# Small matrix products of three token mixers in other array forms, and an issue order that plans by tile size

## The chip, the cores and the metric

The kernel runs on one core of one Trainium2 chip, in float32. The metric is the device time of one execution in microseconds. Before the change three runs took 1665.26, 1686.83 and 1694.75 us; their median is 1686.83 us.

A core has five engines with a queue each: PE multiplies matrices (PEld loads its stationary operand), DVE, ACT and POOL do everything elementwise, SP issues DMAs. PE writes to PSUM, of which this kernel uses eight banks of 128 x 512 float32. The PE array can be addressed as a whole (128 rows x 128 columns, written 128\*128 in the profile) or in part (64\*64, 128\*64, 128\*32, 32\*32 and so on); the part is set by how many partitions the stationary operand spans and how many columns it has. This is called the tile size below. A float32 product shows as two matmul instructions in the trace; a float32r product as one.

## The reference, cut to what matters

One decoder layer over 1024 tokens of 1024 channels:

```
h = x * (1 + scale1) + shift1                  # adaLN, from c
z = h @ w_in                                   # 3984 columns
o = concat(HGRN2(z), GLA(z), RWKV7(z)) @ w_out
x = layer_norm(alpha * x + (1 + gate1) * o)
m = square(relu((x * (1 + scale2) + shift2) @ mlp_w_up)) @ mlp_w_down
x = layer_norm(alpha * x + (1 + gate2) * m)
```

HGRN2 (4 heads of 64) and GLA (6 heads) are gated linear attention: within a chunk, scores of queries and keys with decays between them times values, plus the decayed queries times a state. RWKV-7 (6 heads) is a delta rule, done in chunks of 64 tokens with an inverse of a triangular 64 x 64 matrix for each head and chunk.

## The kernel before

**Dense products.** The tokens are cut into two blocks of 512. Every dense product (projections, MLP) is split into high and low parts and done as three float32r matmuls of 512 or 392 columns (helper `mm3`, L1270 to L1272, tile size 128\*128). ACT makes the high part of a weight slab (L1220), DVE the low part (L1221). They write to PSUM banks `dn` (four) and, in the last part, `tn`.

**Mixers.** `mixers` runs over tiles of 128 tokens, four in each block, RWKV-7 a tile ahead of the attention. For a tile, the steps that the change touches are these.
- `rw_prep` makes AR and BK (for both chunks c and pairs of heads p) and their products (L598): for each c, six float32 products of 64 rows (a half of the partitions holds one head) by 128 columns, tile size 64\*128, into two PSUM banks `mr`. BK holds three parts, k, b and a copy of k that ACT makes (L585), so that one contiguous slice gives the rows in the order that head a needs.
- `rw_prep2` transposes BK (L662): 12 transposes of 64 x 128 in four banks, four ACT copies (L664).
- `rw_invert` (L718 to L750, tile size 32\*32) and `rw_chain` (L770, L775, L781) follow; at the end of the second chunk the outputs y: for each head of a pair, and each chunk d, three products AR x SU (L795, 64\*64), then three E x UV (L798, 128\*64), one bank after the other, one ACT copy each (L800).
- `la_attn` makes the scores level by level. At level 64 (`la_blocks`, L512) it does ten products on 64\*64, heads a = 0 and 1 into two banks `ml`, both on the first 64 columns of the array; level 32 (L521) and the five finer ones (L434) are on 128\*32. Each level is POOL, ACT, DVE, PE and a copy. Then the outputs: for each pair of heads one product of the whole array, decayed queries times the state (L475, 128 columns), and four products of 64 columns, scores times values (L482): for each head the first 64 tokens on 64\*64, the last 64 on 128\*64. ACT copies them out (L484). The state update (transposes L491, products L497) ends the tile.

**Order of issue.** Every engine runs its instructions in the order of its queue. Class `Order` lays that order out when the kernel is built, for all five engines: it simulates them with a cost for each instruction (`cost`), keeps for each engine a heap of instructions that are ready, and takes the one of lowest level, then earliest in the program (`pick`). PSUM banks and buffers are counted (`fits`). If few columns went through PE lately by its count (`behind`), a ready dense product goes first. Levels: the mixers of the first block are at 0, its later projections at 0.5, the second block's projection at 2, the MLP at 3 and up; the second block's mixers at 0 to 6.5. So dense products of a later level fill PE wherever the mixers' products are not ready, one instruction at a time. In `cost`, a PE instruction costs its columns over a rate, and two neighbours on different halves of the array cost half.

Of the kernel before, what the change touches and what calls it, by code (L numbers as in the profile page):

```python
# [19 lines left out]
P = 128  # L20
# [22 lines left out]
# buffers of the mixers' tiles  # L43
WKB = 4
LDB = 2
# of raw and split slabs of weights, of split operands; of late raw tiles
RB, WB, AB, LR = 5, 4, 12, 6
# the last of the groups of 128 columns of adaLN that the first sub-layer's shift and scale take
FIRST = 15
# importance (lower first) of the iterations of each block's mixers  # L50
M0 = (0, 0, 0, 0, 0, 0)
M1 = (0, 0, 3.5, 4.5, 5.5, 6.5)
# of the first block's last projections, the other columns of adaLN, the second block's projection, and the
# first chunk of the MLP, each later chunk being one more
L_Z0, L_ADA, L_Z1, L_MLP = 0.5, 3, 2, 3
# chunks of the first block's MLP that the second block's output projection and its products follow
OUT_AT, MOVE_AT = 4, 6
# tiles of the first layer norm and of the MLP's operand that ACT and Pool take
# [6 lines left out]
# levels of the attention between blocks of 32 tokens, and within them  # L65
# [4 lines left out]
# columns of the array of constants  # L70
# [6 lines left out]
# columns of the array of masks  # L77
# [5 lines left out]
# rows of the array of per-channel vectors  # L83
# [36 lines left out]
class Kern:  # L120
# [13 lines left out]
    # importance of what follows: lower is issued first  # L134
# [7 lines left out]
    # activations of one table set after another: a set's work is issued as a group  # L142
# [30 lines left out]
    # banks of RWKV-7 and of the others  # L173
# [18 lines left out]
    # not before the first columns of adaLN  # L192
# [3 lines left out]
    def setup_mixers(self, masks, vecs, wau, alpha_up, g_up, nrm):  # L196
# [15 lines left out]
        # rows over all partitions: gn_g | gn_b  # L212
# [6 lines left out]
        # lower bounds of HGRN2: softmax over the layers, cumsum less the first  # L219
# [9 lines left out]
        # 1 - k_a  # L229
# [3 lines left out]
        # states  # L233
# [6 lines left out]
        # right factors: zero where the heads of a pair do not meet  # L240
# [12 lines left out]
        # gains of the norms of HGRN2 and GLA  # L253
# [4 lines left out]
    def rw_sig(self, i, src):  # L258
# [13 lines left out]
        # norm of k * k_k  # L272
# [10 lines left out]
        # sigmoids  # L283
# [85 lines left out]
    def la_decay(self, s):  # L369
# [9 lines left out]
        # f * 2**60 below 2**-60, f elsewhere  # L379
# [27 lines left out]
    def la_attn(self, s):  # L407
# [4 lines left out]
        for h in H_OUT + H_LEVELS:  # L412
# [16 lines left out]
            # the four blocks of 32 tokens on the four quarters of the array's columns  # L429
# [11 lines left out]
        # the diagonal  # L441
# [13 lines left out]
        # decayed queries and keys  # L455
# [13 lines left out]
        # outputs  # L469
        for p0, p1 in ((0, 3), (3, 5)):  # L470
            n = p1 - p0
            po = self.lps()
            for p in range(p0, p1):
                c0 = (p - p0) * 128
                nc.tensor.matmul(po[:, c0:c0 + 128], qe[:, p, :], St[:, p, :], start=True, stop=False,  # L475
                                 skip_group_check=True)
                for a in range(2):
                    v0 = p * 128 + 64 * a
                    # the first half of the tokens sees no token of the second
                    for t in range(2):  # L480
                        r = slice(0, 64 + 64 * t)
                        nc.tensor.matmul(po[half[t], c0 + 64 * a:c0 + 64 * a + 64], sc[r, 2 * p + a, half[t]],  # L482
                                         V[r, v0:v0 + 64], start=False, stop=True, skip_group_check=True)
            nc.scalar.copy(o[:, 2 * p0:2 * p1, :], po[:, 0:n * 128].rearrange("p (q d) -> p q d", d=64))  # L484
        # state
# [18 lines left out]
    # the large levels block by block  # L504
    def la_blocks(self, h, e, R):
        nc, sc = self.nc, self.sc
        if h == 64:
            pss = [self.lps() for _ in range(2)]
            for p in range(5):
                for a in range(2):  # L510
                    r = slice(64 * a, 64 * a + 64)
                    nc.tensor.matmul(pss[a][0:64, p * 64:p * 64 + 64], e[r, p * 128:p * 128 + 64], R[r, a, p, :],  # L512
                                     start=True, stop=True)
            for a in range(2):
                nc.scalar.copy(sc[0:64, a::2, 64:128], pss[a][0:64, 0:320].rearrange("p (q t) -> p q t", q=5))
            return
# [27 lines left out]
    def rw_prep(self, i, s):  # L544
# [9 lines left out]
        # decays within each chunk of 64  # L554
# [9 lines left out]
        # kk: k * k_k normalized over the head  # L564
# [9 lines left out]
        BK = self.mt([P, 3, 2, 3, 64], "BK")  # L574
# [3 lines left out]
        nc.vector.tensor_tensor(BKm[:, :, 1, :], c6(b), c6(eb), ALU.mult)  # L578
# [5 lines left out]
        nc.vector.tensor_tensor(BKm[:, :, 0, :], c6(k2), c6(eb), ALU.mult)  # L584
        nc.scalar.copy(BKm[:, :, 2, :], BKm[:, :, 0, :])  # L585
# [3 lines left out]
        # products of the chunks: rows b~, k~ of a head of even number, k~, b~ of an odd one  # L589
        s["E"] = []  # L590
        for c in range(2):
# [3 lines left out]
            for p in range(3):  # L595
                for a in range(2):
                    rr = slice(64 * a, 64 * a + 64)
                    nc.tensor.matmul(pxs[a][:, p * 128:(p + 1) * 128],  # L598
                                     BK[rr, p, c, 1 - a:3 - a, :].rearrange("p x t -> p (x t)"),
                                     AR[rr, p, c].rearrange("p x t -> p (x t)"), start=True, stop=True)  # L600
# [6 lines left out]
    def rw_prep2(self, s):  # L607
# [3 lines left out]
        # bonus coefficients  # L611
# [11 lines left out]
        # gate  # L623
# [4 lines left out]
        # v with the tokens on partitions, opposite to the state's and u's half of each pair  # L628
# [25 lines left out]
        # b~ and k~ with the tokens on partitions  # L654
        s["BKT"] = []
        for c in range(2):
            BT = self.mt([P, 2, 3, 64], "BT", 2)
            for a in range(2):
                rr = slice(64 * a, 64 * a + 64)
                pt = self.mps()  # L660
                for p in range(3):
                    nc.tensor.transpose(pt[:, p * 64:(p + 1) * 64],  # L662
                                        BK[rr, p, c, 1 - a:3 - a, :].rearrange("p x t -> p (x t)"), self.ident[rr, rr])
                nc.scalar.copy(BT[:, a], pt[:, 0:192].rearrange("p (q d) -> p q d", d=64))  # L664
            s["BKT"].append(BT)

    # of an array [m, i, n, j] the parts with n = m
# [5 lines left out]
    def rw_base(self, s):  # L673
        nc = self.nc
        # rows of a head; the inverses go where all but the blocks is zero
# [33 lines left out]
    def rw_invert(self, s):  # L709
        nc = self.nc  # L710
        E, TW = s["E"], s["TW"]
        # blocks of 32, a quarter of the array each
# [907 lines left out]
```

## Time and profile before

| | |
|---|---|
| runs | 1665.26, 1686.83, 1694.75 us; median 1686.83 us |
| profiled execution | its span is 1676.5 us; the page gives no other time for it, and the span is 10.3 us less than the median |
| PE busy | 1565.6 us (93%), 11002 matmuls |
| PEld / DVE / ACT / POOL busy | 1220.9 / 1097.7 / 683.0 / 419.1 us |
| granted TensorE clock, mean | 0.928 |
| PE idle just before an instruction of L434, L475, L598, waiting for DVE or ACT | 17.3, 15.4 and 9.6 us in all |

Read it so: PE is the engine that is nearly always busy; the clock of 0.928 is a mean over stretches at full clock (1.0) and stretches at half (0.5). The 40 slices of the page show the clock under 0.9 only between the seventh and the 24th, that is in the two stretches with the mixers (some 210 to 565 us and 690 to 1060 us), and in the last. From 1060 us on there are only dense products.

### The profile page before, as it was taken

Reading aid. Unit: us, or ns where it says so; the run is one execution under the profiler, and the core shown is the slowest. Engines: PE = TensorE matmul, PEld = TensorE weight load, DVE = VectorE, ACT = ScalarE, POOL = GpSimd, SP = SyncE. Lnnn points to the kernel's source line nnn. Section 1 sums busy time; section 2 is a strip of 40 time slices with the busy share of each in tenths; the row PEclk is TensorE's granted clock in tenths of the full one; section 3 lists DMA queues with packets and bytes.
Section 4 is the critical chain, followed back from the end, with each engine's and each line's share of the span. In section 5 each row is a group of like instructions: output and inputs, shape, how many; then the busy total and the mean of one; then the engine's idle time right before and its main releaser. Section 6 shows DMA issues by size and latency. Waiting matters only on the chain.

```text
span 1676.5 us, 29172 instructions
## 1 busy us (share of the span) xinstructions
PE 1565.6 (93%) x11002; PEld 1220.9 (73%) x11002; DVE 1097.7 (65%) x1877; ACT 683.0 (41%) x1415; POOL 419.1 (25%) x561
## 2 busy tenths in 40 slices
PE   6998988999989998889999999999999999999996
PEld 5887766666667876657667676778888888888885
DVE  8796586666657448875857766555766954444477
ACT  3452343444344655544534543442333333333241
POOL 5224054263434132451452624100000000000003
PEclk9999996787879999898959989999999999999998
DMA  9997542313322456522313131444523643333331
GB/s 310 324 335 232 181 134 68 108 51 110 87 65 86 130 176 194 178 63 77 88 37 105 39 101 44 146 132 130 191 95 94 201 144 96 96 97 96 94 120 50
DMA packets 164892, 214.03 MB, mean 128 GB/s; under 512 B 41456, under 2 KB 91792, under 8 KB 164752
## 3 DMA queue, kind: packets, MB, share of 16 engines
q1 hardware_dynamic: 164752, 212.18, 40.5%
q8 instruction: 86, 1.41, 0.3%
q14 instruction: 54, 0.44, 0.1%
HBM read 180.07 MB, written 32.06 MB: 127 GB/s over the span
## 4 chain that ended last, share of the span: by engine, by line
PE 49%; DVE 6%; DMA 1%; issue 1%; ACT 1%; POOL 1%; SPq 0%; DVEq 0%; ACTq 0%; POOLq 0%
PE dn L1272 10%; PE dn L1271 9%; PE dn L1270 9%; PE tn L1272 4%; PE tn L1271 4%; PE tn L1270 4%; PE ml L482 1%; DVE Rs L425 1%; PE ml L475 1%; PE mr L798 1%; PE mr L795 1%; DVE xt L1401 1%; DVE wl L1221 0%; DMA lnr<-in_ln_b_dram 0%; PE ml L434 0%
## 5 line engine op out<-in xcount | busy, mean ns | idle before, releaser
L1220 ACT CAST wh<-raw 128x512 fp32r<-128x512 f32 (+2 forms) x424 | 253.2, 599 | 558.4 <-PE dn L1272 230.7
L1221 DVE TENSOR_TENSOR wl<-raw,wh 128x512 fp32r<-128x512 f32 (+2 forms) x408 | 284.8, 703 | 274.0 <-ACT wh L1220 246.0
L1270 PE MATMUL dn<-wh,ah 128*128 128x512 f32 (+1 forms) x736 | 288.0, 393 | 6.8 <-DVE xt L1417 3.8
L1271 PE MATMUL dn<-wl,ah 128*128 128x512 f32 (+1 forms) x736 | 288.0, 391 | 2.0 <-DVE wl L1221 2.0
L1272 PE MATMUL dn<-wh,al 128*128 128x512 f32 (+1 forms) x736 | 285.1, 394 | 1.8 <-DVE al L1443 1.8
L1270 PE MATMUL dn<-ah,wh 128*128 128x512 f32 x560 | 236.7, 424 | 19.6 <-ACT ah L1263 11.7
L1271 PE MATMUL dn<-al,wh 128*128 128x512 f32 x560 | 236.7, 423 | 3.2 <-DVE al L1221 1.6
L1272 PE MATMUL dn<-ah,wl 128*128 128x512 f32 x560 | 236.8, 424 | 0.0
L1270 PEld LDWEIGHTS dn<-wh,ah 128*128 128x128 f32 x736 | 140.7, 191 | 36.8 <-ACT wh L1220 3.5
L1271 PEld LDWEIGHTS dn<-wl,ah 128*128 128x128 f32 x736 | 140.3, 191 | 29.6 <-DVE wl L1221 3.4
L1272 PEld LDWEIGHTS dn<-wh,al 128*128 128x128 f32 x736 | 140.0, 191 | 29.5 <-DVE al L1443 3.2
L1270 PEld LDWEIGHTS dn<-ah,wh 128*128 128x128 f32 x560 | 111.8, 200 | 44.4 <-ACT ah L1263 11.7
L1271 PEld LDWEIGHTS dn<-al,wh 128*128 128x128 f32 x560 | 112.0, 200 | 30.3 <-DVE al L1264 4.1
L1272 PEld LDWEIGHTS dn<-ah,wl 128*128 128x128 f32 x560 | 111.8, 200 | 23.6 <-issue 0.4
L416 POOL TENSOR_TENSOR ld<-b 128x640 f32<-128x640 f32 x56 | 76.5, 1373 | 138.0 <-PE ml L512 15.3
L1458 DVE TENSOR_TENSOR xt<-xt,dn 128x512 f32<-128x512 f32 x104 | 67.1, 683 | 52.9 <-PE dn L1272 52.8
L1272 PE MATMUL tn<-ah,wl 128*128 128x512 f32 x256 | 100.8, 394 | 0.0
L1271 PE MATMUL tn<-al,wh 128*128 128x512 f32 x256 | 100.2, 391 | 0.0
L1270 PE MATMUL tn<-ah,wh 128*128 128x512 f32 x256 | 99.6, 389 | 0.0
L1518 POOL TENSOR_SCALAR lnm<-lnm 128x1 f32<-128x1 f32 x3 | 2.1, 684 | 328.5 <-DVE lnm L1516 328.5
L425 DVE TENSOR_TENSOR Rs<-ld,Q 64x320 f32<-64x320 f32 x112 | 82.0, 732 | 2.0 <-ACT ld L157 0.6
L1186 DVE SCALAR_TENSOR_TENSOR xt<-xt,xt 128x1024 f32<-128x1024 f32 x48 | 64.2, 1344 | 16.3 <-DMA xt<-in_ada_wt_dram 16.0
(290 smaller groups left out, 2500.9 us busy)
## 6 DMA issues: line engine op xcount, KB each, us to landing
raw<-in_mlp_w_up_dram SPq DMA_DIRECT2D x128, 256.0 KB
raw<-in_mlp_w_down_dram SPq DMA_DIRECT2D x128, 256.0 KB
xt<-in_ada_wt_dram SPq DMA_DIRECT2D x48, 512.0 KB
raw<-in_w_in_dram SPq DMA_DIRECT2D x64, 256.0 KB
raw<-in_w_in_dram SPq DMA_DIRECT2D x48, 192.0 KB
raw<-in_w_out_dram SPq DMA_DIRECT2D x32, 256.0 KB
raw<-in_w_in_dram SPq DMA_DIRECT2D x32, 196.0 KB
raw<-in_xt_dram SPq DMA_DIRECT2D x24, 256.0 KB
```

What stands on the lines that cost most here:

```text
L416: nc.gpsimd.tensor_tensor(ev, bv, bv[:, :, h - 1:h].broadcast_to([P, 5 * nb, 2 * h]), ALU.subtract)
L425: nc.vector.tensor_tensor(Rv[half[a], a], ev[half[a], :, up], qv[half[a], :, up], ALU.mult)
L475: nc.tensor.matmul(po[:, c0:c0 + 128], qe[:, p, :], St[:, p, :], start=True, stop=False, skip_group_check=True)
L482: nc.tensor.matmul(po[half[t], c0 + 64 * a:c0 + 64 * a + 64], sc[r, 2 * p + a, half[t]], V[r, v0:v0 + 64], start=False, stop=True, skip_gr ...
L795: nc.tensor.matmul(py[half[d], p * 64:p * 64 + 64], AR[rr, p, d, 1, :], s["SU"][d][rr, p, a, :], start=(p == 0), stop=False, skip_group_ch ...
L1186: nc.vector.scalar_tensor_tensor(w, w, 1.0, self.cact, ALU.mult, ALU.mult, accum_out=self.sums[:, q:q + 1])
L1220: nc.scalar.copy(hi[:, 0:n], src)
L1221: (eng or nc.vector).tensor_tensor(lo[:, 0:n], src, hi[:, 0:n].bitcast(F32), ALU.subtract)
L1270: nc.tensor.matmul(ps, lh, rh, start=first, stop=False)
L1271: nc.tensor.matmul(ps, lh, rl, start=False, stop=False)
L1272: nc.tensor.matmul(ps, ll, rh, start=False, stop=last)
L1458: nc.vector.tensor_tensor(acc[t][:, cs], acc[t][:, cs], ps, ALU.add)
```

## The change

Five groups of small products change, and the planner. Comments are dropped too, which moves no instruction.

```diff
 la_attn, outputs
-                    # the first half of the tokens sees no token of the second
-                    for t in range(2):
-                        r = slice(0, 64 + 64 * t)
-                        nc.tensor.matmul(po[half[t], c0 + 64 * a:c0 + 64 * a + 64], sc[r, 2 * p + a, half[t]],
-                                         V[r, v0:v0 + 64], start=False, stop=True, skip_group_check=True)
+                    nc.tensor.matmul(po[:, c0 + 64 * a:c0 + 64 * a + 64], sc[:, 2 * p + a, :], V[:, v0:v0 + 64],
+                                     start=False, stop=True, skip_group_check=True)
 la_blocks, level 64
-            pss = [self.lps() for _ in range(2)]
-            for p in range(5):
-                for a in range(2):
-                    r = slice(64 * a, 64 * a + 64)
-                    nc.tensor.matmul(pss[a][0:64, p * 64:p * 64 + 64], e[r, p * 128:p * 128 + 64], R[r, a, p, :],
-                                     start=True, stop=True)
-            for a in range(2):
-                nc.scalar.copy(sc[0:64, a::2, 64:128], pss[a][0:64, 0:320].rearrange("p (q t) -> p q t", q=5))
+            ps = self.lps()
+            for p, j in ((0, 0), (3, 1), (1, 0), (4, 1), (2, 0)):
+                c0 = (p - 3 * j) * 128
+                for m in range(2):
+                    s0 = 64 * j + 32 * m
+                    nc.tensor.matmul(ps[s0:s0 + 32, c0:c0 + 128], e[:, p * 128 + 32 * m:p * 128 + 32 * m + 32],
+                                     R[:, :, p, :], start=True, stop=True)
+            for j, h0, h1 in ((0, 0, 6), (1, 6, 10)):
+                nc.scalar.copy(sc[0:64, h0:h1, 64:128], ps[64 * j:64 * j + 64, 0:64 * (h1 - h0)]
+                               .rearrange("p (q t) -> p q t", t=64))
 rw_prep (BK has two parts now, b first)
-        nc.scalar.copy(BKm[:, :, 2, :], BKm[:, :, 0, :])
...
-                    nc.tensor.matmul(pxs[a][:, p * 128:(p + 1) * 128],
-                                     BK[rr, p, c, 1 - a:3 - a, :].rearrange("p x t -> p (x t)"),
-                                     AR[rr, p, c].rearrange("p x t -> p (x t)"), start=True, stop=True)
+                for x in range(2):
+                    for a in range(2):
+                        rr = slice(64 * a, 64 * a + 64)
+                        r = slice(64, 128) if a ^ x else slice(0, 64)
+                        nc.tensor.matmul(pxs[a][r, p * 128:(p + 1) * 128], BK[rr, p, c, x, :],
+                                         AR[rr, p, c].rearrange("p x t -> p (x t)"), start=True, stop=True)
 rw_prep2
-            for a in range(2):
-                rr = slice(64 * a, 64 * a + 64)
-                pt = self.mps()
-                for p in range(3):
-                    nc.tensor.transpose(pt[:, p * 64:(p + 1) * 64],
-                                        BK[rr, p, c, 1 - a:3 - a, :].rearrange("p x t -> p (x t)"), self.ident[rr, rr])
-                nc.scalar.copy(BT[:, a], pt[:, 0:192].rearrange("p (q d) -> p q d", d=64))
+            pt = self.mps()
+            for p in range(3):
+                nc.tensor.transpose(pt[:, p * 128:(p + 1) * 128], BK[:, p, c].rearrange("p x t -> p (x t)"), self.ident)
+            pt3 = pt[:, 0:384].rearrange("p (q d) -> p q d", d=128)
+            nc.scalar.copy(BT[:, 0], pt3[:, :, 0:64])
+            for x in range(2):
+                nc.scalar.copy(BT[64 - 64 * x:128 - 64 * x, 1], pt3[64 * x:64 * x + 64, :, 64:128])
 rw_chain, outputs
-            for a in range(2):
-                rr = half[a]
-                py = self.mps()
-                for d in range(2):
-                    for p in range(3):
-                        nc.tensor.matmul(py[half[d], ...], AR[rr, p, d, 1, :], s["SU"][d][rr, p, a, :], ...)
-                    for p in range(3):
-                        nc.tensor.matmul(py[half[d], ...], s["E"][d][:, a, p, 64:128], s["UV"][d][:, p, a, :], ...)
-                nc.scalar.copy(...)
+            pys = [self.mps() for _ in range(2)]
+            for p in range(3):
+                for d, a in ((0, 0), (1, 1), (0, 1), (1, 0)):
+                    nc.tensor.matmul(pys[a][half[d], ...], AR[half[a], p, d, 1, :], s["SU"][d][half[a], p, a, :], ...)
+            for a in range(2):
+                for p in range(3):
+                    for d in range(2):
+                        nc.tensor.matmul(pys[a][half[d], ...], s["E"][d][:, a, p, 64:128], s["UV"][d][:, p, a, :], ...)
+                nc.scalar.copy(...)
```

In the planner, `cost` now charges weight loading with a float32 product, 15 ns with a float32r one, and notes the tile size (`mode`) and the parts of the array (`cells`) of each PE instruction; in `run`, a change of tile size waits until all cells are free and adds 130 ns (`SWITCH`), and an instruction on part of the array holds only its cells, the next may go 20 ns later (`ISSUE`). A predicated copy is charged 1.4 times as much. PE instructions of one tile size other than 128\*128 that follow each other in the program with no other engine's instruction between them form a run:

```diff
+    def runs(self):
+        self.run_of, self.mode, self.cells, last = {}, {}, {}, None
+        for k, i in enumerate(self.ins):
+            if self.eng[k] != PE:
+                last = None
+                continue
+            self.cost(k)
+            if self.mode[k] == (P, P):
+                last = None
+            elif last and self.mode[last[0]] == self.mode[k]:
+                last.append(k)
+            else:
+                last = [k]
...
+        for k, r in self.run_of.items():
+            for m in r[1:]:
+                for d, seen in self.after[m].items():
+                    if d < k:
+                        self.after[k][d] = self.after[k].get(d, 0) or seen
 pick
+            if e == PE and run:
+                x = self.rank[run[0]]
+                if x not in ready[e]:
+                    return None
+                run.pop(0)
+                return take(x)
             if e == PE and behind():
...
+            if e == PE and self.now != (P, P):
+                for x in sorted(ready[e]):
+                    if self.mode[x[1]] == self.now and fits(x[1]):
+                        run.extend(self.run_of.get(x[1], ())[1:])
+                        return take(x)
```

So the first of a run waits for the inputs of all of it and for all its PSUM banks (`fits` sums over the run), the run is then issued unbroken, and after it other ready products of the same tile size come before anything else, unless `behind` asks for a dense one.

## Rows read from the trace of the kernel before

**Rows 1.** Busy time by stage (stretch, length, engines' busy us, clock, DMA share, GB/s).
```profile
210.00:565.00 355.00, 323.61 (x3402) 237.95 (x3402) 230.48 (x421) 160.50 (x393) 148.82 (x205) 0.82 0.30 88
...
690.00:1060.00 370.00, 342.65 (x3529) 250.82 (x3530) 259.66 (x451) 178.29 (x413) 151.91 (x200) 0.87 0.24 70
1060.00:1657.00 597.00, 594.10 (x2612) 484.73 (x2611) 351.45 (x555) 196.70 (x325) 10.65 (x11) 1.00 0.39 121
```

**Rows 2.** The same view, one stretch in the first block's mixers.
```profile
275.90:299.00 23.10, 23.09 (x101) 15.54 (x101) 11.59 (x23) 9.65 (x23) 6.68 (x9) 0.51 0.26 80
```

**Rows 3.** Waits of engines between 210 and 565 us (total us, times, longest).
```profile
POOL ld L468 <- PE ml L475: 41.9, 4, 13.1
ACT wp L800 <- PE mr L798: 31.7, 8, 6.4
```

**Rows 4.** Busy time of L482 alone, one stretch for each tile, first and last of eight.
```profile
275.00:290.00 15.00, 8.33 (x40) 0.55 0.28 84
...
1037.00:1050.00 13.00, 5.20 (x40) 0.85 0.17 51
```

**Rows 5.** Timeline of PE (start, length, operation, count): attention outputs, fourth tile.
```profile
553.46 0.49 PE L475 MATMUL ml<-st,ld 128*128 128x128 f32 x2
553.88 1.73 PE L482 MATMUL ml<-V,sc 64*64 64x64 f32 x14
555.54 0.49 PE L475 MATMUL ml<-st,ld 128*128 128x128 f32 x2
```

**Rows 6.** Timeline of PE: attention outputs, first tile.
```profile
282.79 2.70 PE L482 MATMUL ml<-V,sc 64*64 64x64 f32 x14
285.42 0.80 PE L475 MATMUL ml<-st,ld 128*128 128x128 f32 x2
```

**Rows 7.** Timeline of PE: first product off the whole array; last before dense products alone.
```profile
95.81 0.37 PE L291 MATMUL mr<-zm,wau 64*128 64x128 f32 x1
...
1050.44 0.80 PE L497 MATMUL ml<-V,ld 128*64 128x64 f32 x20
1051.17 0.50 PE L1271 MATMUL dn<-al,wh 128*128 128x512 f32 x1
```

**Rows 8.** Timeline of PE: outputs y of RWKV-7, third tile.
```profile
458.34 0.56 PE L795 MATMUL mr<-SU,AR 64*64 64x64 f32 x6
458.82 0.56 PE L798 MATMUL mr<-UV,E 128*64 128x64 f32 x6
```

**Rows 9.** Timeline of PE: small products between dense ones, first tile.
```profile
248.33 0.33 PE L770 MATMUL mr<-SU,E 128*64 128x64 f32 x2
248.59 0.50 PE L1271 MATMUL dn<-al,wh 128*128 128x512 f32 x1
248.93 0.40 PE L1272 MATMUL dn<-ah,wl 128*128 128x512 f32 x1
249.25 0.25 PE L434 MATMUL ml<-Rs,ld 128*32 128x32 f32 x2
249.43 0.56 PE L770 MATMUL mr<-SU,E 128*64 128x64 f32 x10
249.92 0.46 PE L434 MATMUL ml<-Rs,ld 128*32 128x32 f32 x32
250.46 0.56 PE L775 MATMUL mr<-sm,TW 64*64 64x64 f32 x12
```

**Rows 10.** Groups of PE instructions by line and shape (count, busy us, mean ns, idle before).
```profile
L662 PE MATMUL mr<-consts,BK 64*128 64x64 f32 x96 | 15.3, 296 | 0.8 <-ACT BT L664 0.6 <-DVE bon L651 0.3
...
L631 PE MATMUL mr<-consts,zm 128*128 128x128 f32 x24 | 4.6, 308 | 0.0
```

**Rows 11.** Waits of PE over the whole span (total us, times, longest).
```profile
PE mr L598 <- ACT BK L585: 9.6, 4, 3.1
```

**Rows 12.** The instructions of L585 (duration min/median/max in ns).
```profile
L585 ACT COPY BK<-BK x8: 509/512/515, 113.3 to 919.0; 128x384 f32<-128x384 f32 x8
```

**Rows 13.** Timeline of PE: products of the chunks and of level 64, sixth tile.
```profile
813.55 0.94 PE L598 MATMUL mr<-AR,BK 64*128 64x128 f32 x12 [3.14 <-ACT BK L585]
814.42 1.15 PE L512 MATMUL ml<-Rs,ld 64*64 64x64 f32 x20
```

## What the change will do to the time: the prediction

> **What bounds the kernel now.** First the busy times by stage [rows 1]: PE is busy for 324 of 355 us in the mixers of the first block, for 343 of 370 us in those of the second, for 594 of 597 us in the dense stretch behind. No other engine comes near: DVE has 230 and 260 us. So the kernel is as long as PE's work, and the question for every edit is what it takes from PE. The second thing to see there is the clock: 0.82 and 0.87 in the two mixer stretches against 1.00 in the dense one. The clock has two levels here, 1.2 and 2.4 GHz, so 0.82 means that 36% of 355 us (128 us) ran at the lower one, and 0.87 that 26% of 370 us (96 us) did: 224 us in all. Rows 2 [rows 2] show what PE did in such a stretch: busy for 23.09 of 23.10 us, with 101 instructions, most of them small products.
>
> Next the waits [rows 3]: in the first block POOL waited 41.9 us for L475 and ACT 31.7 us for L798. Slow small products thus hold the mixers' own chain as well as PE.
>
> Last the timeline of PE. In the attention outputs 14 instructions of L482, which alternate between two tile sizes, take from 553.88 to 555.54, 119 ns each, and L475's pair between them 0.42 us [rows 5]; in the first tile, at the lower clock, 14 take 2.63 us, 188 ns each [rows 6]. And each stretch on one tile size has a fixed cost: two instructions of L770 hold PE for 0.26 us, ten for 0.49 us, so one more costs 0.03 us and the stretch itself 0.20 us; the dense product after it takes 0.34 us where its neighbours take 0.23 [rows 9]. Counted over all of PE's instructions, the array changes size 861 times, first at 95.81 us, and 1051.17 us is the last change of the mixers [rows 7]; 585 stretches are off the whole array, 155 of them of L482, 82 of L795 and L798, 30 of L662.
>
> **The parts.** Eight tiles of tokens; prices at full clock, then weighted.
>
> *Attention outputs (L475, L482).* A tile now: 40 x 0.119 + 5 x 0.42 = 6.9 us at full clock, x 188/119 = 10.8 us at the lower. The eight stretches of L482 had clocks from 0.52 to 0.98, mean 0.70, the first and last 0.55 and 0.85 [rows 4], so 60% at the lower: 8 x (0.4 x 6.9 + 0.6 x 10.8) = 74 us. After, 20 instructions of the whole array with 64 columns take the place of the 40, and L475's ten have no change of size around them. No row has such an instruction. From above: L475's 210 ns with 128 columns and a change on either side. From below: L497, 64 columns on half-width tiles, 20 in 0.73 us, 37 ns [rows 7]. I take half of L475's, 105 ns, for it streams half the columns through the same whole array, and 150 ns for L475 itself: 20 x 0.105 + 10 x 0.15 = 3.6 us, 7.2 at the lower clock. With the share as now 46 us, with 30% at the lower 37 us: between them, **-32 us**. Ends: +7 us (210 ns for all, share as now) and -55 us (37 ns).
>
> *Outputs y (L795, L798).* Six instructions take 0.48 us [rows 8], 80 ns each, and all six of one group lie on the same part of the array. 48 a tile: 3.8 us. After, 24 on 64\*64 go round four parts, then 24 on 128\*64 round two. L775 (64\*64, two parts) takes 0.56 us for 12, 47 ns, L770 (128\*64, two parts) 49 ns [rows 9]: 2.3 us. With the stage's clock (some 30% at the lower, factor 1.17) 8 x 1.5 x 1.17 = **-14 us**; ends 0 and -21 us, the latter if the four parts give L434's 17 ns (32 in 0.54 us [rows 9]). Both banks `mr` are now held at once; before, the second could be filled while ACT copied the first. That is one copy more to wait for in a tile, under 0.5 us, covered by dense products.
>
> *Transposes (L662).* 96 instructions cost 15.3 us, 159 ns each; 48 of the whole array at L631's 4.6/24 = 192 ns [rows 10] make 9.2: **-6 us**. ACT gets six copies a tile for four and loses L585's; it is busy for 160 of 355 us [rows 1], so I cost that at nothing; uncovered it would be 1 us a tile.
>
> *The copy L585.* It lasts 0.51 us [rows 12] and PE waited for it four times, 9.6 us [rows 11]; the product on DVE that it copies ends just before it, and that is what is late next. So not 9.6 but 4 x 0.5 = **-2 us**.
>
> *Chunk products (L598) and level 64 (L512).* L598 takes 0.87 us for 12 now; after, 24 of 128 columns go round four parts. L434, 32 columns on four parts, 17 ns, is the lower bound, four times that, 68 ns, the upper; at 40 ns they cost 0.96 us: **0**, ends -7 and +12 us over 16 groups. L512 takes 54 to 57 ns for each of 20 [rows 13]; after, the same count with 128 columns on four parts, 0.8 for 1.1 us: **-3 us**, ends -6 and +2. It holds one bank `ml` instead of two and has the tile size of the next levels.
>
> *Order.* The forms take away 267 stretches and bring back 16; 318 others stay. In the program a tile's small products come in some 27 groups, 216 for eight tiles: about 100 stretches fewer at 0.20 us, 0.31 where a dense product stood behind: **-20 us**; ends -45 (groups of one size meet often) and +10. This adds a wait: a run's first instruction waits for the last input of the run and for all its banks. Behind it in PE's queue stands everything, dense products too, but the planner puts a run there only when it sees the inputs as ready. The same simulation also lays out DVE, ACT, POOL and SP anew, the DMAs of the inverses and of the weight slabs among them; DMA is at 0.30 and 0.24 of its time in these stretches [rows 1], which leaves room, so nothing for that; without that room a weight slab's wait would be added to PE.
>
> *Clock.* Small products lose about a quarter of their time. If the 224 us at the lower clock shrink alike, by 56 us, 28 us come back; half of it is in the terms above. **-15 us**; the end on the good side is -50.
>
> **Sum.** -32 - 14 - 6 - 2 - 3 - 20 - 15 = -92 us. The profiled span is 1676.5 us, 10.3 us under the median of the runs; the same step from the median gives 1687 - 92 = **1595 us**. With the ends of single terms this case covers 1540 to 1630 us.
>
> **The rivals.**
>
> *The whole array is not cheaper.* Against the step on L482 stands a trace price too: 64-column products on part of the array run at 37 ns (L497), a third of what I charge for the whole. If those 210 ns of L475 are the real price, the term turns from -32 to +7: 1595 + 39 = 1634 us. Chance 0.12. The Trainium skill, "TensorEngine Tiling (Array Packing)", section "Theoretical Speedup", has it that way: a dimension of 64 or less, put on tiles, goes up to twice as fast, so L482 and L662 should have stayed on parts. By that rule the time would be this rival's. L482's 119 ns, no quicker than my price for the whole, speaks against it where sizes alternate.
>
> *PE's freed time goes idle in the first block.* There the dense products left to fill are few, and a chain of POOL, ACT, DVE and PE sets the pace; DVE is busy for 65% of it. Then only the second block, filled by the MLP, pays: half of 92, 1641 us. For it: PE's 31 idle us in that stretch. Against it: rows 3, where POOL and ACT wait for just these products. Chance 0.13.
>
> *Unbroken small products hold the clock down.* Place: the two mixer stretches. Rows 2 show PE busy all the time and still at half clock, so busy alone doesn't keep the clock; runs that no dense product may break could make such stretches longer. Each further us at the lower clock costs half a us of work. The other terms give 77 us; it takes 154 us more at the lower clock to eat them, 222 more (446 of the 725 us) to be slower by 2%. At 480 us: (480 - 224)/2 - 77 = +51, 1738 us. Against it: the rule that puts dense products first when few columns went through stands ahead of the new one, and the worst stretches are those of L482, which shrink. Chance 0.08.
>
> *The order gives it back.* The planner's new prices move everything; if the new order fits the chip worse by some 80 us of stalls, the time is that of before, 1665 to 1690 us. Idle time of PE in the mixer stretches is 59 us now; it would have to double. Chance 0.12.
>
> **The numbers.** Forecast 0.55, rivals 0.12, 0.13, 0.08, 0.12. A measurement of this kernel tells about 2% (34 us) from no change: 1653 us. The forecast, most of the first rival and two thirds of the second lie below: faster 0.74. The fourth and what is left of the others: same 0.20; slower 0.06. The range 1520 to 1660 leaves out the third and nearly all of the fourth, and the good ends of the clock and order terms.
>
> **What would show it.** L482's successor with 160 instructions of 128\*128 at about 105 ns; y in 2.3 us a tile; changes of tile size well under half of 861; clock above 0.85 in the first mixer stretch; both mixer stretches shorter by 35 to 50 us, the dense stretch after them unchanged. I am wrong in the mechanism if PE's idle time in the mixers grows by more than 30 us, or the clock falls.

## The result, and the profile after

The changed kernel takes 1602.80 us (median of four runs, 1601.35 to 1604.74); the kernel before, run beside it, 1680.66. The ratio is 0.956, with a 95% interval of 0.951 to 0.961: faster by 4.4%. The forecast was 1595 us, range 1520 to 1660. The profiled span went from 1676.5 to 1603.0 us.

The busy times by stage (stretch, length, busy us of PE, PEld, DVE, ACT, POOL, clock, DMA share, GB/s) of the changed kernel, against [rows 1]; first, of the kernel before, the stretch between its mixers, which [rows 1] leaves out:

```profile
565.00:690.00 125.00, 113.62 (x572) 90.02 (x570) 86.22 (x151) 65.03 (x127) 37.09 (x59) 1.00 0.63 196
...
210.00:500.00 290.00, 235.50 (x3273) 177.64 (x3272) 233.36 (x417) 157.14 (x384) 151.81 (x206) 0.88 0.34 99
500.00:640.00 140.00, 132.24 (x698) 109.10 (x697) 87.21 (x152) 72.11 (x143) 37.60 (x59) 0.99 0.60 182
640.00:975.00 335.00, 279.79 (x3481) 215.24 (x3480) 256.69 (x447) 173.60 (x404) 149.52 (x198) 0.89 0.28 81
975.00:1583.00 608.00, 602.36 (x2651) 489.77 (x2648) 356.15 (x564) 203.56 (x339) 12.47 (x12) 1.00 0.38 120
```

The mixer stretches shrank by 65 and 35 us, the dense stretch behind them is as full as before. That is more than the whole span lost, because dense work moved out of the mixers (577 and 701 dense instructions there became 479 and 666): the stretch between them has 698 instructions of PE in 140 us where it had 572 in 125, and the last one 2651 where it had 2612. But see what became of PE in the mixers: it is idle for 54.5 of 290 and 55 of 335 us, where it was 31 and 27. DVE has the same work in less time and is busy for 80% of the first stretch (65% before). PE's longest waits (total us, times, longest) are for DVE. The first was 17.3 us before; the other two are new, for before PE waited 0.8 us in front of L662 and 9.6 for ACT's copy in front of L598:

```profile
PE ml L434 <- DVE Rs L425: 22.2, 18, 3.9
PE mr L661 <- DVE bon L652: 19.0, 5, 6.6
PE mr L600 <- DVE BK L585: 13.6, 6, 3.2
```

The changed groups, by line and shape (count, busy us, mean ns of one, idle before), first of the kernel before:

```profile
L482 PE MATMUL ml<-V,sc 64*64 64x64 f32 x160 | 32.5, 297 | 0.0
L482 PE MATMUL ml<-V,sc 128*64 128x64 f32 x160 | 32.3, 302 | 0.0
...
L475 PE MATMUL ml<-st,ld 128*128 128x128 f32 x80 | 25.3, 412 | 15.4 <-DVE ld L460 15.4
...
L798 PE MATMUL mr<-UV,E 128*64 128x64 f32 x192 | 22.9, 256 | 0.0
L598 PE MATMUL mr<-AR,BK 64*128 64x128 f32 x192 | 22.5, 337 | 9.9 <-ACT BK L585 9.6
L795 PE MATMUL mr<-SU,AR 64*64 64x64 f32 x192 | 22.2, 250 | 2.3 <-DVE UV L778 2.3
```

and of the changed kernel, where L480 is the old L482, L600 the old L598, L661 the old L662, L800 the old L798:

```profile
L480 PE MATMUL ml<-V,sc 128*128 128x64 f32 x160 | 23.6, 268 | 0.0
L600 PE MATMUL mr<-AR,BK 64*64 64x128 f32 x384 | 19.8, 311 | 16.9 <-DVE BK L585 13.6 <-DVE BK L579 3.2
L475 PE MATMUL ml<-st,ld 128*128 128x128 f32 x80 | 19.3, 336 | 3.5 <-DVE ld L460 3.5
L661 PE MATMUL mr<-consts,BK 128*128 128x128 f32 x48 | 11.1, 354 | 20.1 <-DVE bon L652 19.0 <-ACT BT L665 1.0
L512 PE MATMUL ml<-Rs,ld 128*32 128x128 f32 x160 | 10.0, 367 | 0.7 <-DVE Rs L425 0.6
L800 PE MATMUL mr<-UV,E 128*64 128x64 f32 x192 | 8.1, 236 | 0.0
L795 PE MATMUL mr<-SU,AR 64*64 64x64 f32 x192 | 6.1, 246 | 1.3 <-DVE SU L786 1.3
```

The mean of one is its length from start to end, and neighbours overlap, so prices are read from starts. From here on each PE instruction is charged the time to the start of the next, less the idle time in front of that one. The timeline of the changed kernel (start, length, count), attention outputs of the fourth tile at full clock:

```profile
489.89 0.44 PE L475 MATMUL ml<-st,ld 128*128 128x128 f32 x2
490.17 0.56 PE L480 MATMUL ml<-V,sc 128*128 128x64 f32 x4
490.56 0.44 PE L475 MATMUL ml<-st,ld 128*128 128x128 f32 x2
490.84 0.56 PE L480 MATMUL ml<-V,sc 128*128 128x64 f32 x4
491.20 0.42 PE L1328 MATMUL dn<-wh,al 128*128 128x392 f32 x1
```

Four of L480 take 0.36 to 0.39 us, 90 to 98 ns each; a pair of L475 0.28. And RWKV-7's outputs, against [rows 8]:

```profile
468.63 0.85 PE L795 MATMUL mr<-SU,AR 64*64 64x64 f32 x24
469.42 0.92 PE L800 MATMUL mr<-UV,E 128*64 128x64 f32 x24
470.26 0.50 PE L1326 MATMUL dn<-ah,wh 128*128 128x512 f32 x1
```

24 in 0.79 us and 24 in 0.84, 33 and 35 ns each, in two stretches where there were eight or more.

Added up that way over the whole span, with every kernel of the study (medians and ratios from the runs, each ratio against the kernel before as it ran beside that kernel, with medians of 1677 to 1681 us; the other columns from the one profiled execution, in us of PE; "dense" are the instructions of `mm3`, "small" all others, "lower" is the time at the lower clock):

| kernel | median | ratio, 95% interval | dense | small | idle | lower | changes of tile size |
|---|---|---|---|---|---|---|---|
| before | 1680.66 | 1 | 1234 | 331 | 96 | 243 | 861 |
| changed | 1602.80 | 0.956 (0.951-0.961) | 1216 | 220 | 152 | 161 | 345 |
| forms only | 1604.98 | 0.954 (0.950-0.959) | 1229 | 261 | 101 | 168 | 614 |
| planner only | 1673.93 | 0.998 (0.996-1.000) | 1241 | 270 | 147 | 195 | 678 |
| changed, no runs | 1648.03 | 0.980 (0.977-0.984) | 1250 | 249 | 133 | 168 | 621 |
| changed, old attention outputs | 1637.41 | 0.975 (0.972-0.979) | 1220 | 254 | 152 | 195 | 542 |
| changed, new PE prices alone | 1671.88 | 0.994 (0.990-0.998) | 1273 | 270 | 113 | 212 | 760 |
| changed, no preference | 1595.85 | 0.950 (0.945-0.956) | 1214 | 218 | 147 | 146 | 363 |
| changed, other prices raised | 1547.99 | 0.921 (0.916-0.927) | 1213 | 204 | 116 | 101 | 355 |
| forms only, other prices raised | 1571.54 | 0.935 (0.929-0.942) | 1216 | 247 | 91 | 97 | 643 |
| changed, old y | 1624.01 | 0.969 (0.964-0.974) | 1227 | 240 | 147 | 184 | 413 |
| changed, DVE's price raised | 1563.12 | 0.932 (0.928-0.936) | 1208 | 206 | 130 | 96 | 360 |
| changed, prices raised threefold | 1573.41 | 0.939 (0.934-0.943) | 1220 | 212 | 128 | 155 | 337 |
| other prices raised, no preference | 1551.41 | 0.925 (0.920-0.930) | 1211 | 205 | 120 | 99 | 366 |

So the 73.5 us between the first two spans are 111 us less of small products, 18 less of dense ones, and 56 us more of idle time.

### The profile page after: what moved, and what is told of

Same layout as the page of the kernel before. It is cut to its first block, busy times and chain, and to the rows that moved or that the text cites. A ratio compares the mean times of both kernels' runs of the same rounds, so it can differ in the third digit from the quotient of the medians.

```text
span 1603.0 us, 29184 instructions
## 1 busy us (share of the span) xinstructions
PE 1436.2 (90%) x10986; PEld 1144.5 (71%) x10986; DVE 1099.2 (69%) x1877; ACT 687.0 (43%) x1423; POOL 418.0 (26%) x561
## 4 chain that ended last, share of the span: by engine, by line
PE 51%; DVE 11%; POOL 6%; DMA 3%; issue 3%; ACT 3%; SPq 0%; DVEq 0%; POOLq 0%; ACTq 0%
PE dn L1328 11%; PE dn L1326 11%; PE dn L1327 11%; PE tn L1328 5%; PE tn L1327 5%; PE tn L1326 4%; DVE Rs L425 1%; POOL btw L699 1%; POOL btm L697 1%; DVE wl L1277 1%; DVE zm L269 1%; POOL ld L416 1%; DMA lnr<-in_ln_b_dram 1%; DVE ld L420 1%; DVE xt L1457 1%
## 5 line engine op out<-in xcount | busy, mean ns | idle before, releaser
L1277 DVE TENSOR_TENSOR wl<-raw,wh 128x512 fp32r<-128x512 f32 (+2 forms) x408 | 289.0, 712 | 339.7 <-ACT wh L1276 304.6
L1328 PE MATMUL dn<-ah,wl 128*128 128x512 f32 x560 | 233.2, 418 | 2.2 <-DVE wl L1277 2.1
L425 DVE TENSOR_TENSOR Rs<-ld,Q 64x320 f32<-64x320 f32 x112 | 77.2, 690 | 3.3 <-ACT ld L157 2.3
L157 ACT ACTIVATE ld<-ld 128x320 f32<-128x320 f32 (+1 forms) x120 | 55.0, 491 | 42.9 <-POOL ld L416 41.0
```

Of the source, the lines that this page charges most:

```text
L157: ins = nc.scalar.activation(out, in_, func, **kw)
L425: nc.vector.tensor_tensor(Rv[half[a], a], ev[half[a], :, up], qv[half[a], :, up], ALU.mult)
L1277: (eng or nc.vector).tensor_tensor(lo[:, 0:n], src, hi[:, 0:n].bitcast(F32), ALU.subtract)
L1328: nc.tensor.matmul(ps, ll, rh, start=False, stop=last)
```

## The experiments

**Forms and planner apart.** The first kernel has the new forms and class `Order` of before, the second the forms of before and the new `Order`.

> The new array forms of the five groups, with the planner of before. In the changed kernel the five groups take 67.5 us of PE against 159.9 before (start to start), so about 92 us less, and PE's idle time is 152 us against 96. Theory (the forms bring most of the gain; idle time gives part back): L475 and L480 together under 40 us, the y group under 25 us, 1615 to 1640 us. Rival (the order of issue brings most of it, the forms would still be cut up by changes of tile size): the y group over 30 us, 1650 us or more.

> The new planner with the array forms of before. Theory (forms first): the attention outputs keep their alternation of tile sizes, L475 and L482 stay near 75 us; the other groups save some 20 to 30 us, y a part more; 1640 to 1670 us. Rival (order first): 1625 us or less.

The forms alone give the whole gain: 1604.98 us; the two ratios, 0.954 and 0.956, can't be told apart. They save 71 us of small products: L475 with L480 34.3 us (76.3 before), y 20.4 (39.4), L661 6.6 (13.2); L600 and L512 hardly move. Groups of this kernel:

```profile
L480 PE MATMUL ml<-V,sc 128*128 128x64 f32 x160 | 28.2, 308 | 0.0
L475 PE MATMUL ml<-st,ld 128*128 128x128 f32 x80 | 21.4, 365 | 19.5 <-DVE ld L460 19.4
L795 PE MATMUL mr<-SU,AR 64*64 64x64 f32 x192 | 11.9, 251 | 2.4 <-DVE SU L786 1.5 <-DVE UV L779 0.9
L800 PE MATMUL mr<-UV,E 128*64 128x64 f32 x192 | 10.9, 254 | 0.0
```

The planner alone gives 0.2%: it saves 61 us of small products and pays 51 us of idle time and 7 us of dense time. Both times came outside what I expected, the forms 10 us below it, the planner 4 us above. Nor did L475 and L482 stay near 75 us with the planner alone: they took 57.4, for fewer of them ran at the lower clock (75 of 400 against 228). On top of the forms it does the same again: 41 us of small and 13 of dense products against 51 us of idle time.

**Is a group's PE time worth its time?** The old attention outputs, then the old outputs y, put back into the changed kernel.

```diff
-                    nc.tensor.matmul(po[:, c0 + 64 * a:...], sc[:, 2 * p + a, :], V[:, v0:v0 + 64], ...)
+                    for t in range(2):
+                        r = slice(0, 64 + 64 * t)
+                        nc.tensor.matmul(po[half[t], c0 + 64 * a:...], sc[r, 2 * p + a, half[t]], V[r, v0:v0 + 64], ...)
```

> The changed kernel with the attention outputs of before (two products of 64 columns for each head on 64*64 and 128*64 instead of one on the whole array). Theory (term of 47 us, PE bound): 30 to 50 us slower than the changed kernel, 1633 to 1653 us. Rival (freed PE time went idle in the mixers, so giving it back costs little): under 15 us slower, with idle time falling by 25 us or more.

> The changed kernel with the outputs y of RWKV-7 in the order of before (three products of one head and chunk after another on one part of the array, one bank after the other). y takes 13.1 us of PE in the changed kernel (28 and 38 ns an instruction at full clock) and 39.4 in the kernel before. Theory (PE bound, the term is its PE time): 15 to 30 us slower than the changed kernel, 1618 to 1633 us, the two lines at 60 ns or more. Rival (with the new order of issue y's old form costs little, its price before came from being cut up by dense products): the lines under 50 ns, under 10 us slower.

Old attention outputs cost 34.6 us (1637.41 against 1602.80), and PE's time for L475 and L482 rises from 29.6 to 63.4 us, by 33.8; idle time stays at 152. Old y costs 21.2 us, PE's time rises by 22.2. Both pay one for one, so neither term went idle. Groups of the kernel with the old attention outputs:

```profile
L482 PE MATMUL ml<-V,sc 64*64 64x64 f32 x160 | 28.6, 273 | 0.0
L482 PE MATMUL ml<-V,sc 128*64 128x64 f32 x160 | 28.5, 274 | 0.0
...
L475 PE MATMUL ml<-st,ld 128*128 128x128 f32 x80 | 21.7, 364 | 6.5 <-DVE ld L460 6.5
```

and of the one with the old y (L796 and L799 are L795 and L798 of before):

```profile
L796 PE MATMUL mr<-SU,AR 64*64 64x64 f32 x192 | 19.9, 244 | 0.0
L799 PE MATMUL mr<-UV,E 128*64 128x64 f32 x192 | 19.8, 246 | 0.0
```

With the new planner the old forms keep nearly their old price: 122 ns an instruction of L482 at full clock (125 before), 81 of y (88 before). For y this shows that the form sets it, not the cutting up: its 64 groups of six now run in one piece each, where they were in 82 pieces before. For L482 it shows less: its neighbours in the program differ in tile size, so a run is one product, and it still comes in 150 pieces of mostly one product (155 before). That the old products, sorted by tile size, would be as cheap as the new form was not run. An estimate from y's price speaks against it: those of one size all lie on one part of the array, so 320 instructions at 81 ns would take 26 us, against 16 for 160 of L480 at 100 ns.

**What in the planner makes idle time?** First its parts: no runs (`run_of` left empty); new PE prices alone (also no preference; what stays is the whole new account of PE, with its parts of the array and its changes of tile size); no preference.

```diff
-        self.run_of = {k: r for k, r in self.run_of.items() if r[0] == k}
+        self.run_of = {}
...
-            if e == PE and self.now != (P, P):
+            if e == PE and self.now != (P, P) and False:
```

> The changed kernel without unbroken runs: a small product is planned when its own inputs are there; prices and the preference for the tile size at hand stay. Theory A (the wait of a run's first instruction for the last input made the added 56 us of idle time): idle time falls from 152 to 110 us or less, changes of tile size rise from 345, time 1580 to 1600 us. Rival B (idle time comes from the other engines' chain, DVE above all, busy for 80% of the first mixer stretch now): idle stays within 15 us of 152, time 1603 to 1625 us.

> The new forms with the planner's new prices alone: no unbroken runs, no preference for the tile size at hand. The forms alone (planner of before) took 1605 us with 101 us idle and 261 us of small products; the whole change 1603 with 152 and 220. Theory P (the new prices make the plan quick on PE while its prices for DVE, ACT and POOL stay too low, so PE comes too early and waits): idle already 130 us or more here, time 1610 to 1640 us. Theory R (the runs and the preference make the idle time): idle near 100 us, time 1595 to 1610 us.

> The changed kernel with unbroken runs but without the preference for the tile size at hand. Without the runs and with the preference it took 1648 us. Theory (the preference lets late products of one size go ahead of more urgent ones and costs idle time; the runs alone save changes of tile size): idle under 140 us, 1585 to 1600 us. Rival (the preference makes no difference once runs are unbroken): 1600 to 1608 us.

On the first two neither theory came: idle time fell by 19 and 39 us only, and both kernels were far slower, 1648 and 1672 us. The new PE prices alone lose 67 us against the forms with the old prices, 44 of it in dense products. A stretch of its timeline shows what the plan did:

```profile
242.96 0.21 PE L730 MATMUL mr<-TW,sm 32*16 32x16 f32 x2
243.10 0.51 PE L1328 MATMUL dn<-ah,wl 128*128 128x512 f32 x1
243.53 0.21 PE L730 MATMUL mr<-TW,sm 32*16 32x16 f32 x2
243.67 0.49 PE L1326 MATMUL dn<-ah,wh 128*128 128x512 f32 x1
244.10 0.22 PE L730 MATMUL mr<-TW,sm 32*16 32x16 f32 x4
244.25 0.50 PE L1327 MATMUL dn<-al,wh 128*128 128x512 f32 x1
```

One dense instruction after every two or four small ones, at a clock of 1.00; the first two dense ones hold PE for 0.43 us each, against 0.23 in the dense stretch of the changed kernel (2651 instructions in 608 us). Runs forbid this: with them and the same prices, that is in the kernel without the preference, it takes 1596 us, 76 less. The preference for the tile size at hand adds nothing on top of the runs: without it 1595.85 us, which is in the theory's range, but the interval of the ratio overlaps that of the changed kernel, and idle time is 147 us, not under 140. Without the runs it is worth 24 us (1648 against 1672).

**The prices of the other engines.** `cost` prices a product of L425 on DVE (64 x 320 elements) at 68 + 320/0.96 = 401 ns. The trace of the changed kernel has 690 in the mean (first line; the second has the shortest, the median and the longest, in ns):

```profile
L425 DVE TENSOR_TENSOR Rs<-ld,Q 64x320 f32<-64x320 f32 x112 | 77.2, 690 | 3.3 <-ACT ld L157 2.3
L425 DVE TENSOR_TENSOR Rs<-ld,Q x112: 472/489/2096, 222.5 to 960.7; 64x320 f32<-64x320 f32 x112
```

The mean hides two cases. The 49 that ran with POOL idle took 490 ns at most; the 63 that overlap an instruction of POOL took 850 in the mean, and all 32 that are longer than 520 ns are among these. So no one price fits all: 24% over 401 ns is 498, the price of those that run alone, and 72% over it is 690, the mean. If the plan believes DVE to be quicker than it is, it queues PE's next product too early and PE waits. So `cost` was scaled, first for the changed kernel, then for the forms with the planner of before:

```diff
+SCALE = {DVE: 1.24, ACT: 1.18, POOL: 1.26}
...
+        d, c = self.price(n)
+        return d * SCALE.get(self.eng[n], 1), c
```

> The changed kernel, with the planner's prices for DVE, ACT and POOL raised by 24, 18 and 26%; only the order of issue changes. Example: a product of L425 on DVE is planned at 68 + 320/0.96 = 401 ns, the trace has 690 ns. Theory P (the added idle time is PE waiting for engines that are slower than planned): idle falls from 152 to 115 us or less, small products stay within 10 us of 220, 1560 to 1590 us. Rival (idle comes from the chain of the mixers itself, whatever the plan): idle within 15 us of 152, 1595 to 1615 us.

> The new forms with the planner of before, its prices for DVE, ACT and POOL raised alike. Theory P: there PE is priced too slow already (its small products at four times their columns), which hides the other engines' low prices, and idle is only 101 us; raising them gains little: 1590 to 1612 us. Rival (any better price helps alike): as much gained as by the same step in the changed kernel.

No instruction changes, only the order: 1547.99 us, 55 less than the changed kernel, with idle time down from 152 to 116. That is theory P's idle time to 1 us, and a time below the one it gave, since small products lost 16 us too, more than the 10 it allowed. All of PE's waits for DVE fall from 93 to 70 us, those for ACT from 49 to 38. In front of L434 and L661 they fall from 22.2 and 19.0 us, in front of L512 they rise from 0.6:

```profile
PE ml L434 <- DVE Rs L425: 13.6, 16, 2.3
PE ml L512 <- DVE Rs L425: 12.1, 4, 5.4
PE mr L661 <- DVE bon L652: 7.7, 4, 3.9
```

By stage:

```profile
210.00:490.00 280.00, 242.22 (x3374) 190.37 (x3374) 238.22 (x431) 162.33 (x396) 152.29 (x203) 0.95 0.39 115
...
620.00:925.00 305.00, 270.79 (x3474) 206.11 (x3476) 264.50 (x459) 175.68 (x412) 157.88 (x201) 0.95 0.28 80
```

The clock is 0.95 in both mixer stretches, and DVE is busy for 85 and 87% of them. With the old planner the same step gives 33 us. That is neither what theory P gave (1571.54 us, under its 1590) nor the rival's 55, and it is made of other things: idle time falls by 10 only, small products by 14, dense by 13, and the time at the lower clock from 168 to 97 us. So the idle time is the part that belongs to the new planner; that the clock gains with either I had not expected.

> The changed kernel with the planner's price for DVE alone raised by 24%. All three raised gave 1548 us with 116 us idle, against 1603 and 152. Theory (DVE, busy for 80% of the first mixer stretch, is the engine that PE waits for): at least two thirds of the gain, 1545 to 1567 us. Rival (the prices of ACT and POOL, which stand ahead of DVE in every level of the attention, matter as much): 1570 to 1600 us.

> The changed kernel with the three prices raised three times as far: DVE 72, ACT 54, POOL 78% over the planner's own. Theory (what helps is that the plan comes near the chip): the plan is now as far off on the other side, and the gain shrinks: 1560 to 1600 us. Rival (what helps is any push of the other engines' work ahead of PE's): 1548 us or less.

> The changed kernel with the raised prices (24, 18, 26%) and without the preference for the tile size at hand, which took 1596 us for 1603 by itself. If the two gains add: 1535 to 1545 us, the fastest version so far. If the raised prices have taken away what the preference spoiled: 1545 to 1555 us.

DVE's price alone brings 40 of the 55 us. Prices three times as far raised bring 29: more of the push is not better, which speaks against "the other engines first" whatever the size. It fits a plan near the chip, if near means the duration of an instruction that runs undisturbed: for L425 the smaller step gives that, the larger one the mean. Only these two sizes were run for all three prices, so where the best lies stays open. Without the preference the raised prices give 1551.41 us, the same as with it. The fastest version of the study is thus the changed kernel with raised prices, 1548 us, ratio 0.921.

## Why the prediction was right, and where its steps failed

**The bound** was right for the forms: PE, in the mixers. Two groups put back cost what they take of PE, and the dense stretch behind did not change. It was not the whole of it under the new planner, where PE's saved time went idle and better prices for the other engines gave 55 us.

**Attention outputs, -32 us: -47 measured.** The prices were right: 100 ns an instruction at full clock for 105, 139 for 150 for L475. The share at the lower clock was not: 30 of the 240 instructions, where I took 30 to 60%. In the forms-only kernel 90 of 240 run at the lower clock and the term is -42.

**Outputs y, -14: -26.** With the old planner they cost 49 and 43 ns, as the 47 and 49 that I took from L775 and L770, and the term is -19; unbroken they fall to 28 and 38 ns. The term passes my end of -21 on both sides of it: y took 39.4 us before where I had 36, and 13.1 after where that end has 15.

**Transposes, -6: -6.2. Chunk products, 0: -2.4**, 43 ns for my 40. **Level 64, -3: -0.4**, 36 ns for my 40, but 100 of its 160 instructions now run at the lower clock.

**The copy L585, -2: the wrong sign.** PE now waits 16.8 us for the two products on DVE that make BK (L579 and L585 of the changed kernel) where it waited 9.6 for the copy; with the forms alone it waits 13.5. The copy was the last link of a chain that DVE sets. That PE, with the rest of its work shorter, comes to it earlier is likely, but not shown.

**Order, -20: nothing.** This is the step that failed. The changes of tile size fell by 516, 247 of them with the forms alone, and the order did save PE 41 us of small and 13 us of dense products. But I cost the waits that the new order adds at nothing, because the planner "sees the inputs as ready"; it sees them too early. Its 51 us of idle time took nearly all of it back; raising the planner's prices for the other engines took 36 us of idle time away again. My own sign of a wrong mechanism came true here: PE's idle time in the mixers grew by 51 us (from 59 to 110), where I had set 30 as the limit. It is much like my second rival, PE's freed time going idle, for the planner's part, though not by the place that I gave: idle time grew by 23 us in the first block and by 28 in the second, which the MLP was to fill. For the forms it is false, idle time grew by 5 us.

One price in this term was read too low. The 0.23 us that I set beside the 0.34 is not in [rows 9]; it is the price in the dense stretch (594 us for 2612 instructions). In [rows 9] the dense instruction in front of a change takes 0.32 us. So a stretch of small products between dense ones costs them some 0.2 us in all, not 0.11, as the 0.43 us above also has it.

**Clock, -15: right in sign.** The time at the lower clock fell from 243 to 168 us with the forms alone and to 161 in the whole change. What that is worth can't be read off by itself: most of it is in the groups' terms above. Dense products gained 5 us with the forms alone and 18 in the whole change, part of it from fewer changes of tile size beside them.

For forms and clock together -72 was forecast (-57 and -15), and the forms alone came to -72. There two errors met: the five groups gave 68 us for 55, the dense products 5 us for the clock's 15. For the order -20 was forecast, and about 0 came. That is why the time came a little over the forecast, and why it was near it although the term of the order failed.

**The other rivals.** *The whole array is not cheaper*: false, 100 ns an instruction with half the count against 122. So the "up to 2x" for a dimension of 64 or less on tiles, in the Trainium skill's "TensorEngine Tiling (Array Packing)", "Theoretical Speedup", gave nothing for L482, whose two tile sizes alternate. For y, on tiles round four parts, the trace agrees: 28 ns an instruction, against 100 for 64 columns on the whole array. *Unbroken small products hold the clock down*: false, with 345 changes of size in place of 861 the time at the lower clock fell by 82 us. *The order gives it back*: true of the planner by itself, at 0.998, and nearly so for PE's idle time in the mixers, which almost doubled; but not for the kernel, since the forms' gain stayed.

What stays open: why the new PE prices alone make the plan put a dense product between every few small ones; by what way raised prices keep the clock up, also with the old planner; and what L482 would cost in its old form, sorted by tile size. No run isolates any of them.

## What to carry to other kernels

Where small products alternate between tile sizes, first look for a form with one size, even if it uses the array less; where they don't depend on each other, issue them round the parts of the array. In this kernel an order planned with new prices for one engine, and prices of the others left too low, turned saved work into waiting. Three prices raised towards the traced durations were worth 33 us under the old rules and 55 under the new, the new rules by themselves 2. And look at a traced duration before it becomes a price: a mean can mix two cases.

## What the runs showed that was not expected

The new prices for PE alone made the same instructions 4% slower (1605 to 1672 us); a higher price for DVE alone made them 2.5% faster (1603 to 1563).

Instructions on four parts of the array, 64 columns each, go at 28 ns one after the other; on the same part, 81 ns.

In the changed kernel L425's product on DVE took 490 ns at most when POOL was idle, and 850 in the mean, up to 2.1 us, beside an instruction of POOL.
